# A decoder mixer on one core: low parts by accumulating transfer, layer 0's memory keys as split products, and three convolution taps moved from TensorE to VectorE

## The chip, the cores and the metric

The kernel runs as one program on one core of a Trainium2 chip. The core has TensorE (matrix products, "PE" in the profile; its weight loads are "PEld"), VectorE ("DVE"), ScalarE ("ACT"), GpSimd ("POOL"), SyncE ("SP", which here only issues transfers) and 16 DMA engines. The metric is the device time of one execution in microseconds (us), the median over several runs.

## The reference, cut to what matters

Two residual layers over a sequence of 512 positions with 1024 channels, all in f32; each layer has a mixer, a cross-attention into 256 memory tokens and a gated FFN. The change lies in layer 0's mixer and in the work that is done beside it:

```python
z = h @ w_in                                   # 1024 -> 512 (pooling) + 512 + 512 (gated convolution)
u, glu_a, glu_b = split(z)
pooled = [window_mean_minus_self(u_group_i, w) for w in (2, 4, 8, 16)]
ya = einsum(pooled, pool_w) * pool_scale
gl = glu_a * sigmoid(glu_b)
cv = causal_dwconv(gl, dw_w) + dw_b            # 31 taps on each of 512 channels
yb = silu(layernorm(cv, ln_g, ln_b))
x = x + concatenate([ya, yb]) @ w_out
# for the cross-attention of both layers, from the same memory tokens:
k, v = split(rmsnorm(mem, norm_mem_g) @ wkv)
```

## The kernel before

Activations lie transposed: a tile has 128 channels on the partitions and 512 positions along the row. To keep f32 accuracy, an operand `a` is split into a high part (a cast to the type fp32r) and a low part `a - high`; a product is then three TensorE products in fp32r, high x high, high x low and low x high (`mm3`, lines 179 to 181). A weight tile is 128 x 1024 f32 (512 KB). `load_raw` fetches it by a transfer of SP's queue into one of 4 buffers `wr`; `load_w` has ScalarE cast the high part (line 173, "wh") and VectorE subtract the low part (line 174, "wl"), each in one of 3 buffers, asked for 40 places ahead of its turn.

A second way to the low part is there and is used in the FFN only: ScalarE writes minus the high part's source, and a transfer of POOL's queue adds the weights from memory a second time.

```python
def early_parts():
    hi = wp.tile([P, WCOLS], F32R, tag="wh1", name=uid("wh1"), bufs=2)
    lo = wp.tile([P, WCOLS], F32R, tag="wl1", name=uid("wl1"), bufs=2)
    return hi, lo

def low_by_dma(lo, raw, src):
    act.mul(lo, raw, -1.0)                     # line 166; lo is fp32r: it keeps minus the rounded value
    pool.dma_start(lo, src, accum_op=ALU.add)  # line 167
```

The mixer does this, in the order of the code: twelve projection tiles of 24 products each (`opening`, then `project`; b and a halves of four channel groups, then the four pooling groups); layer 0's memory keys (8 tiles) and values (8 tiles, with the four products of the pooling map between them); layer 1's memory keys and values (16 tiles), kept in memory for later; the first half of the output projection, whose operand is `ya` (8 x 12 products, in 16 steps); its second half, whose operand is `yb`. Layer 0's keys are taken as f32 products of the raw weights with the raw memory tile (`native`, line 362); layer 1's are split products.

The depthwise convolution runs beside all that. Three channel groups and most taps of the fourth are VectorE instructions of 128 x up to 512 elements (line 934, `convolve`). The taps in `PE_TAPS` of the fourth group are TensorE products with a diagonal matrix (`tap_products`, line 945; ScalarE builds the diagonal, line 944), added to the rest at line 950. The code deals out VectorE's taps by counts, `PACE`, a few after every weight tile; `left[0]` counts those still open. When none is open, the stages of `normalise` (the LayerNorm over the channels and the swish, lines 952 to 981) are called one after the other at the steps that `LATE` gives.

The program text is not the order in which the engines run. A planner takes, for each engine, the ready instruction that stands first in the text (an instruction can be given a place ahead of its turn, as above), and readiness includes a free buffer. Each engine then runs its list in that order.

Of the kernel before, what the change touches and what calls it, by code (L numbers as in the profile page):

```python
# [19 lines left out]
P = 128  # L20
T = 512
TB = T // P
D = 1024
KD = D // P
# [25 lines left out]
WCOLS = 1024  # L50
SLOTS = 55
AHEAD = 40
FIN_AHEAD = 2
K_NATIVE = (True, False)
MEM_AT = (3, 6, 8)
MLA_AHEAD = 3
PE_TAPS = [1] + list(range(31 - 4, 31))
PE_PACE = 2
PACE = (3, 3, 2, 3)
MEM1_AT = 10  # L60
# [5 lines left out]
EARLY = 150  # L66
# [39 lines left out]
def kernel(ctx: ExitStack, tc: tile.TileContext, a):  # L106
    nc = tc.nc
    vec, act, pe, pool, sp = nc.vector, nc.scalar, nc.tensor, nc.gpsimd, nc.sync
# [10 lines left out]
    def uid(s):  # L119
        count[0] += 1  # L120
        return f"{s}{count[0]}"

    def slot(name, dt=F32, shape=(P, T)):
        return sl.tile(list(shape), dt, tag="s", name=uid(name))

    def bank(name="ps", shape=(P, T)):
        return pp.tile(list(shape), F32, tag="ps", name=uid(name))

    def small(name, shape, bufs=2, dt=F32):
        return sm.tile(list(shape), dt, tag=name, name=uid(name), bufs=bufs)  # L130

    def f(t):
        return t.bitcast(F32)
# [6 lines left out]
    def col(name, i=0, n=1):  # L140
        c = _COLS[name] + i
        return con[:, c:c + n]
# [5 lines left out]
    def load_raw(src, n):  # L148
        raw = wp.tile([P, WCOLS], F32, tag="wr", name=uid("wr"), bufs=4)
        sp.dma_start(raw[:, :n], src)  # L150
        return raw

    def parts():
        hi = wp.tile([P, WCOLS], F32R, tag="wh", name=uid("wh"), bufs=3)
        lo = wp.tile([P, WCOLS], F32R, tag="wl", name=uid("wl"), bufs=3)
# [10 lines that stand above are left out]
        act.mul(lo, raw, -1.0)  # L166
        pool.dma_start(lo, src, accum_op=ALU.add)  # L167

    def load_w(src, n):
        raw = load_raw(src, n)  # L170
        hi, lo = parts()
        with tc.high_priority(offset=AHEAD):
            act.copy(hi[:, :n], raw[:, :n])  # L173
            vec.tensor_tensor(lo[:, :n], raw[:, :n], f(hi[:, :n]), ALU.subtract)  # L174
        return hi, lo

    def mm3(ps, ah, al, bh, bl, first, last, more=False):

        pe.matmul(ps, ah, bh, start=first, stop=False, skip_group_check=more)  # L179
        pe.matmul(ps, ah, bl, start=False, stop=False, skip_group_check=more)  # L180
        pe.matmul(ps, al, bh, start=False, stop=last, skip_group_check=more)  # L181
# [153 lines left out]
                src = self.raw[k // 2][:, k % 2, :]  # L335
                vec.tensor_tensor(src, src, mem_rb, ALU.mult)

    def memory_gain(layer, memn, mg, mh):
        for i in range(KD // 2):
            m = slot("mg", shape=(P, 2, MEM))  # L340
            h = slot("mh", F32R, (P, 2, MEM))
            l = slot("ml", F32R, (P, 2, MEM))
            for j in range(2):
                act.activation(m[:, j, :], memn[i][:, j, :], AF.Identity,
                               scale=col("norm_mem_g", layer * KD + 2 * i + j))
            act.copy(h, m)
            vec.tensor_tensor(l, m, f(h), ALU.subtract)
            for j in range(2):
                mg.append(m[:, j, :])
                mh.append((h[:, j, :], l[:, j, :]))  # L350
            yield

    def memory_kv(layer, mg, mh, keep, native, kt, vt):

        for hd in range(HX):
            ps = bank("kx", (P, 2, MEM))
            for j in range(2):
                src = a["xa_wk"][layer, 2 * hd + j]
                if native:
                    w = load_raw(src, D)  # L360
                    for k in range(KD):
                        pe.matmul(ps[:, j, :], w[:, k * P:(k + 1) * P], mg[k], start=k == 0, stop=k == KD - 1)
                else:
                    Linear(src, KD, ps[:, j, :]).run(mh, 0, KD)
                yield
            kt.append(keep(ps, (P, 2, MEM)))
        for half in range(2):
            ps = [bank("vx") for _ in range(MB)]
            for kk in range(KD // 2):
                wh, wl = load_w(a["xa_wv"][layer, half, kk], 2 * T)  # L370
                for j in range(2):
                    k = 2 * kk + j
                    c = slice(j * T, (j + 1) * T)
                    for m in range(MB):
                        h, l = mh[k]
                        s = slice(m * P, (m + 1) * P)
                        mm3(ps[m], h[:, s], l[:, s], wh[:, c], wl[:, c], k == 0, k == KD - 1)
                yield
            for m in range(MB):
                vt[m].append(keep(ps[m], (P, T)))  # L380
# [490 lines left out]
    def mixer(norm, nxt):  # L871
        mem = Memory()
# [45 lines left out]
        def convolve():  # L918

            todo = [list(range(CONV_K)) for _ in range(CT - 1)] + [[s for s in range(CONV_K) if s not in PE_TAPS]]  # L920
            last = -1
# [16 lines left out]
        def tap_products():  # L938

            ps = bank("tap")  # L940
            i = CT - 1
            for n, s in enumerate(PE_TAPS):
                dg = small("dg", [P, P], bufs=4)
                act.activation(dg, ident, AF.Identity, scale=col("conv_dw_w", (CONV_K - 1 - s) * CT + i))
                pe.matmul(ps[:, s:], dg, gl[i][:, :T - s], start=n == 0, stop=n == len(PE_TAPS) - 1)
                yield
            while left[0]:
                yield
            s = PE_TAPS[0]
            vec.tensor_tensor(cv[i][:, s:], cv[i][:, s:], ps[:, s:], ALU.add)  # L950
# [32 lines left out]
        cv = [sl.tile([P, T], F32, tag="cv", name=uid("cv"), bufs=CT) for _ in range(CT)]  # L983
        left = [CONV_K * CT - len(PE_TAPS)]
        conv = convolve()

        def taps(n):
            for _ in range(min(n, left[0])):
                next(conv)
# [18 lines left out]
        for n, (kind, i) in enumerate(order):  # L1008
            if n == 2:
                lin.run(norm.h, 0, RB_K)  # L1010
                rb = norm.wide()
                wait.append((kind, i, lin.run(norm.h, RB_K, KD)))
            else:
                wait.append((kind, i, (project if n else opening)(base[kind] + i)))
            if n == 0:
                act.dma_start(con[:, KD:], a["con"][:, KD:])
            if n == 1:
                lin = Linear(a["pc_in"][base[order[2][0]] + order[2][1]], KD)
                lin.load(0)
                norm.r = row_rate(a["xN"], TB, "rx")  # L1020
            elif n > 1:
                if n == MEM_AT[0]:
                    mem.rate()
                if n == MEM_AT[1]:
                    mem.scale()
                if n == MEM_AT[2]:
                    scaled = [], []
                    for _ in memory_gain(0, mem.raw, *scaled):
                        pass
                while len(wait) > 1:  # L1030
                    finish(*wait.pop(0))
                if gl:
                    taps(PACE[0])
        kv = [], [[] for _ in range(MB)]
        products = tap_products()
        steps = memory_kv(0, *scaled, keep_slot, K_NATIVE[0], *kv)
        scaled = [], []
        gains = memory_gain(1, mem.raw, *scaled)
        for n, _ in enumerate(steps):
            if n == 0:  # L1040
                finish(*wait.pop(0))
# [11 lines left out]
        kv = [], [[] for _ in range(MB)]  # L1053
# [2 lines left out]
        late = normalise()  # L1056

        def filler():
            for _ in memory_kv(1, *scaled, keep_whole, K_NATIVE[1], *kv):
                yield 2  # L1060
            for m in range(KD):
                lin = Linear(a["pc_out"][m][:, :CT * P], CT)
                lin.run(cat, 0, CT // 2)
                yield 1
                vec.tensor_tensor(x[m], x[m], lin.run(cat, CT // 2, CT), ALU.add)
                yield 1
# [3 lines left out]
        for step in filler():  # L1070
            if left[0]:
                if step == 2 or left[0] % 2:
                    taps(PACE[3])
                if not left[0]:
                    for _ in products:
                        pass
            else:
                due -= 1
            if not left[0] and due <= 0 and stage < len(LATE):
                next(late, None)  # L1080
                due = LATE[stage]
                stage += 1
        out.append(kv)
        taps(left[0])
        for _ in products:
# [365 lines left out]
```

## Time and profile before

| | |
|---|---|
| median of 3 runs | 1383.85 us (1382.74 to 1384.0) |
| the profiled execution: time, span | 1383.12 us, 1381.3 us |
| TensorE busy, mean granted clock | 1352.6 us (98%), 0.993 |
| VectorE, ScalarE, POOL busy | 1020.0, 748.8, 52.9 us |
| layer 0's memory keys on TensorE | 75.9 to 107.6 us |
| layer 1's memory keys and values | 132.7 to 177.7 us |
| output projection, first half | 177.7 to 203.3 us |

Times of day are counted from the span's start. A row of a stretch has, for each engine, its busy time and in brackets the number of its instructions, then the granted TensorE clock as a share of full speed, the share of the 16 DMA engines that is busy, and GB/s. A row of the order in time has start, length, engine, line, operation, output and inputs, and in square brackets what the engine waited for. Matmul lengths overlap: the rate is read from their starts.

### The profile page before, as it was taken

Reading aid. Unit: us, or ns where it says so; the run is one execution under the profiler, and the core shown is the slowest. Engines: PE = TensorE matmul, PEld = TensorE weight load, DVE = VectorE, ACT = ScalarE, POOL = GpSimd, SP = SyncE. Lnnn points to the kernel's source line nnn. Section 1 sums busy time; section 2 is a strip of 40 time slices with the busy share of each in tenths; the row PEclk is TensorE's granted clock in tenths of the full one; section 3 lists DMA queues with packets and bytes.
Section 4 is the critical chain, followed back from the end, with each engine's and each line's share of the span. In section 5 each row is a group of like instructions: output and inputs, shape, how many; then the busy total and the mean of one; then the engine's idle time right before and its main releaser. Section 6 shows DMA issues by size and latency. Waiting matters only on the chain.

```text
span 1381.3 us, 20270 instructions
## 1 busy us (share of the span) xinstructions
PE 1352.6 (98%) x7756; PEld 1168.1 (85%) x7756; DVE 1020.0 (74%) x1897; ACT 748.8 (54%) x1264; POOL 52.9 (4%) x71
## 2 busy tenths in 40 slices
PE   8999999999989999999999999999999999999997
PEld 6888978888879999999887776888887899999987
DVE  6999989554787777776869775755549777777765
ACT  6416456445655555554447786644556555555433
POOL 0000000001100000000000000000011000000000
PEclk9999999999999999999999999999999999999999
DMA  9335634118835545553321113321486455555421
GB/s 327 99 104 188 217 104 151 61 38 207 184 91 130 159 124 138 134 137 94 106 81 50 43 47 107 107 77 61 124 188 124 130 132 143 134 136 144 111 73 62
DMA packets 57265, 168.01 MB, mean 122 GB/s; under 512 B 6480, under 2 KB 8144, under 8 KB 57168
## 3 DMA queue, kind: packets, MB, share of 16 engines
q1 hardware_dynamic: 47664, 135.55, 30.6%
q0 software_dynamic: 7776, 28.32, 12.3%
q10 hardware_dynamic: 1728, 2.86, 0.6%
q8 instruction: 60, 0.98, 0.3%
q14 instruction: 37, 0.30, 0.1%
HBM read 162.50 MB, written 4.19 MB: 121 GB/s over the span
## 4 chain that ended last, share of the span: by engine, by line
PE 88%; DVE 8%; ACT 2%; issue 1%; DMA 0%; SPq 0%; DVEq 0%; ACTq 0%
PE lin L179 11%; PE lin L181 11%; PE lin L180 11%; PE xyz L179 8%; PE xyz L180 8%; PE xyz L181 8%; PE down L180 4%; PE down L179 4%; PE down L181 4%; DVE cv L934 3%; PE s L1273 1%; PE mpv L1310 1%; DVE wl L174 1%; PE t L1298 1%; PE vx L180 1%
## 5 line engine op out<-in xcount | busy, mean ns | idle before, releaser
L179 PE MATMUL xyz<-th,wh 128*128 128x256 f32 x816 | 230.8, 284 | 10.6 <-ACT q L737 10.6
L181 PE MATMUL xyz<-th,wl 128*128 128x256 f32 x816 | 231.5, 284 | 0.0
L180 PE MATMUL xyz<-tl,wh 128*128 128x256 f32 x816 | 231.3, 284 | 0.0
L173 ACT CAST wh<-wr 128x1024 fp32r<-128x1024 f32 (+3 forms) x120 | 112.7, 944 | 161.8 <-issue 60.6
L179 PE MATMUL lin<-hh,wh 128*128 128x512 f32 x432 | 171.0, 396 | 5.9 <-ACT hh L286 5.9
L179 PEld LDWEIGHTS xyz<-th,wh 128*128 128x128 f32 x816 | 155.7, 192 | 23.2 <-ACT q L737 14.9
L180 PE MATMUL lin<-hl,wh 128*128 128x512 f32 x432 | 169.7, 393 | 0.0
L181 PE MATMUL lin<-hh,wl 128*128 128x512 f32 x432 | 169.2, 392 | 0.2 <-DVE wl L174 0.2
L180 PEld LDWEIGHTS xyz<-tl,wh 128*128 128x128 f32 x816 | 156.8, 192 | 7.1
L174 DVE TENSOR_TENSOR wl<-wr,wh 128x1024 fp32r<-128x1024 f32 (+3 forms) x120 | 130.1, 1086 | 42.4 <-ACT wh L173 40.9
L181 PEld LDWEIGHTS xyz<-th,wl 128*128 128x128 f32 x816 | 156.7, 192 | 0.0
L565 DVE TENSOR_TENSOR wl<-ws,wh 128x1024 fp32r<-128x1024 f32 x68 | 83.3, 1225 | 61.4 <-ACT wh L564 47.9
L564 ACT CAST wh<-ws 128x1024 fp32r<-128x1024 f32 x68 | 71.3, 1049 | 103.9 <-PE xyz L180 101.3
L179 PE MATMUL down<-fh,dwh 128*128 128x512 f32 x256 | 101.9, 398 | 1.2 <-ACT dwh L218 1.2
L180 PE MATMUL down<-fl,dwh 128*128 128x512 f32 x256 | 102.0, 398 | 0.0
L181 PE MATMUL down<-fh,dwl 128*128 128x512 f32 x256 | 100.5, 393 | 0.5 <-DVE dwl L219 0.5
L179 PEld LDWEIGHTS lin<-hh,wh 128*128 128x128 f32 x432 | 81.6, 189 | 22.3 <-ACT hh L286 6.2
L180 PEld LDWEIGHTS lin<-hl,wh 128*128 128x128 f32 x432 | 81.5, 189 | 18.5 <-DVE hl L287 2.7
L181 PEld LDWEIGHTS lin<-hh,wl 128*128 128x128 f32 x432 | 81.5, 189 | 17.5 <-DVE wl L174 0.6
L167 POOL DMA_DIRECT2D wl<-in_ffn_up x54 | 46.9, 868 | 1058.2 <-ACT wl L166 1058.2
L934 DVE SCALAR_TENSOR_TENSOR cv<-a,con,cv 128x509 f32<-128x509 f32 (+25 forms) x115 | 79.4, 726 | 0.1
L670 ACT ACTIVATE c<-c 128x512 f32<-128x512 f32 x44 | 27.8, 632 | 58.5 <-DVE c L669 58.3
(404 smaller groups left out, 3152.1 us busy)
## 6 DMA issues: line engine op xcount, KB each, us to landing
wr<-in_ffn_up SPq DMA_DIRECT2D x88, 512.0 KB, 4.1
wl<-in_ffn_up POOLq DMA_DIRECT2D x54, 512.0 KB, 5.7
dr<-in_ffn_down SPq DMA_DIRECT2D x64, 256.0 KB, 4.2
wr<-in_xa_wk SPq DMA_DIRECT2D x16, 512.0 KB, 3.5
wr<-in_xa_wv SPq DMA_DIRECT2D x16, 512.0 KB, 4.3
wr<-in_xa_wq SPq DMA_DIRECT2D x16, 512.0 KB, 3.5
wr<-in_xa_wo SPq DMA_DIRECT2D x16, 512.0 KB, 3.5
wr<-in_ffn_down SPq DMA_DIRECT2D x16, 384.0 KB, 3.3
```

Source lines behind the costliest of these rows:

```text
L167: pool.dma_start(lo, src, accum_op=ALU.add)
L173: act.copy(hi[:, :n], raw[:, :n])
L174: vec.tensor_tensor(lo[:, :n], raw[:, :n], f(hi[:, :n]), ALU.subtract)
L179: pe.matmul(ps, ah, bh, start=first, stop=False, skip_group_check=more)
L180: pe.matmul(ps, ah, bl, start=False, stop=False, skip_group_check=more)
L181: pe.matmul(ps, al, bh, start=False, stop=last, skip_group_check=more)
L564: act.copy(hi[:, :n], raw)
L565: vec.tensor_tensor(lo[:, :n], raw, f(hi[:, :n]), ALU.subtract)
L670: act.activation(c, c, AF.Silu)
L934: vec.scalar_tensor_tensor(cv[i][:, s:], gl[i][:, :T - s], w, cv[i][:, s:], ALU.mult, ALU.add)
L1273: pe.matmul(ps[i], q[:, i * P:(i + 1) * P], k[:, :P * (i + 1)], start=True, stop=True)
L1298: pe.transpose(banks[b][:, c:c + P], prob[n][i][:, j * P:(j + 1) * P], ident)
```

## The change

1. In the mixer, from behind the opening tile to the end of the first half of the output projection, every second full-width weight tile that `load_w` fetches (the first, the third, ...) gets its low part by the accumulating transfer, in the two early buffers, with its instructions asked for 150 places ahead.
2. Layer 0's memory keys are taken as split products, as layer 1's are; the native form is gone.
3. `PE_TAPS` shrinks from five taps (1, 27 to 30) to two (1, 30). The three others are done by VectorE.

```diff
-K_NATIVE = (True, False)
-PE_TAPS = [1] + list(range(31 - 4, 31))
+PE_TAPS = [1, 30]
...
+    relief = [False, 0]
+
     def load_w(src, n):
         raw = load_raw(src, n)
+        if relief[0] and n == WCOLS:
+            relief[1] += 1
+            if relief[1] % 2:
+                with tc.high_priority(offset=EARLY):
+                    hi, lo = early_parts()
+                    act.copy(hi, raw)
+                    low_by_dma(lo, raw, src)
+                return hi, lo
         hi, lo = parts()
...
-    def memory_kv(layer, mg, mh, keep, native, kt, vt):
+    def memory_kv(layer, mh, keep, kt, vt):
...
-                if native:
-                    w = load_raw(src, D)
-                    for k in range(KD):
-                        pe.matmul(ps[:, j, :], w[:, k * P:(k + 1) * P], mg[k], start=k == 0, stop=k == KD - 1)
-                else:
-                    Linear(src, KD, ps[:, j, :]).run(mh, 0, KD)
+                Linear(src, KD, ps[:, j, :]).run(mh, 0, KD)
...
+            if n == 0:
+                relief[0] = True
             if n == 1:
                 lin = Linear(a["pc_in"][base[order[2][0]] + order[2][1]], KD)
...
-        steps = memory_kv(0, *scaled, keep_slot, K_NATIVE[0], *kv)
+        steps = memory_kv(0, scaled, keep_slot, *kv)
...
+        relief[0] = False
         out.append(kv)
         taps(left[0])
```

More of the change, by code (lines that the diff above doesn't have):

```diff
@@ L336, in scale, with memory_gain @@
                 vec.tensor_tensor(src, src, mem_rb, ALU.mult)
-    def memory_gain(layer, memn, mg, mh):
+    def memory_gain(layer, memn, mh):
         for i in range(KD // 2):
@@ L348, in memory_gain @@
             for j in range(2):
-                mg.append(m[:, j, :])
                 mh.append((h[:, j, :], l[:, j, :]))
             yield
-    def memory_kv(layer, mg, mh, keep, native, kt, vt):
+    def memory_kv(layer, mh, keep, kt, vt):
         for hd in range(HX):
@@ L1026, in mixer @@
                 if n == MEM_AT[2]:
-                    scaled = [], []
-                    for _ in memory_gain(0, mem.raw, *scaled):
+                    scaled = []
+                    for _ in memory_gain(0, mem.raw, scaled):
                         pass
@@ L1035, in mixer @@
         products = tap_products()
-        steps = memory_kv(0, *scaled, keep_slot, K_NATIVE[0], *kv)
-        scaled = [], []
-        gains = memory_gain(1, mem.raw, *scaled)
+        steps = memory_kv(0, scaled, keep_slot, *kv)
+        scaled = []
+        gains = memory_gain(1, mem.raw, scaled)
         for n, _ in enumerate(steps):
@@ L1058, in filler @@
         def filler():
-            for _ in memory_kv(1, *scaled, keep_whole, K_NATIVE[1], *kv):
+            for _ in memory_kv(1, scaled, keep_whole, *kv):
                 yield 2
```

## The prediction

> **What bounds the kernel now.** I read the page's busy shares and its chain first, then busy times by stage.
>
> ```profile
> PE 1352.6 (98%) x7756; PEld 1168.1 (85%) x7756; DVE 1020.0 (74%) x1897; ACT 748.8 (54%) x1264; POOL 52.9 (4%) x71
> PE 88%; DVE 8%; ACT 2%; issue 1%; DMA 0%; SPq 0%; DVEq 0%; ACTq 0%
> ```
>
> TensorE bounds the whole, with VectorE on 8% of the chain. The stretches below are: opening, projections (to 75.9), layer 0 memory keys (to 107.6), its values (to 132.7), layer 1 keys (to 155.9) and values (to 177.7), first half of the output projection (to 203.3). The last two rows are FFN stretches that are used later.
>
> ```profile
> core 0: us, PE busy (x) PEld busy (x) DVE busy (x) ACT busy (x) POOL busy (x), PEclk, DMA share, GB/s
> 0.00:20.00 20.00, 13.94 (x44) 9.05 (x45) 10.82 (x13) 15.27 (x29) 0.71 (x6) 1.00 0.92 338
> 20.00:40.00 20.00, 20.00 (x92) 16.57 (x91) 15.46 (x36) 11.22 (x22) 0.00 (x0) 1.00 0.81 278
> 75.90:107.60 31.70, 31.70 (x139) 26.20 (x138) 31.70 (x67) 6.23 (x10) 0.00 (x0) 1.00 0.36 116
> 107.60:132.70 25.10, 25.02 (x110) 20.08 (x110) 25.10 (x34) 17.21 (x27) 0.20 (x1) 1.00 0.56 190
> 132.70:155.90 23.20, 23.20 (x194) 23.16 (x193) 23.20 (x30) 11.13 (x14) 0.00 (x0) 1.00 0.75 226
> 155.90:177.70 21.80, 21.80 (x98) 18.05 (x97) 19.93 (x27) 9.61 (x12) 0.00 (x0) 1.00 0.56 183
> 177.70:203.30 25.60, 24.13 (x108) 19.06 (x107) 20.60 (x44) 13.63 (x23) 0.00 (x0) 1.00 0.29 94
> 325.00:380.00 55.00, 55.00 (x248) 45.50 (x248) 34.00 (x67) 33.65 (x45) 7.79 (x9) 1.00 0.88 196
> 401.70:406.60 4.90, 4.90 (x20) 4.61 (x21) 3.23 (x6) 1.36 (x3) 0.00 (x0) 0.50 0.36 119
> ```
>
> From 20 to 178 us TensorE never rests, and VectorE is full until 156. Both bind, so relief of VectorE alone brings little: only removed TensorE work shortens this stretch, if the operands stay on time.
>
> **Keys as split products.** The native form issues two records per product.
>
> ```profile
> 79.57 1.83 PE L945 MATMUL tap<-a,dg 128*128 128x511 f32 x4
> 90.58 17.43 PE L362 MATMUL kx<-mg,wr 128*128 128x256 f32 x80
> L179 PE MATMUL kx<-mh,wh x64: 278/283/283, 132.9 to 155.6; 128*128 128x256 f32 x64
> ```
>
> 80 records from 90.2 to 107.6 are 0.217 us each (the record's 17.43 us over 80 gives the same), so the 128 of layer 0 cost 27.8 us. Layer 1 already takes the split form: 3 x 64 products in 23.2 us, 0.121 each. Gain 27.8 - 23.2 = 4.6 us.
>
> **Taps.** The keys' stretch holds 31.7 us; less 27.8, five tap products took 3.9, or 0.78 each. The row above agrees (four records, two products, 1.83 us with the last one's tail). Three removed: -2.3 us. Together -6.9 us of TensorE work. Their three diagonal builds leave ScalarE, which is idle there.
>
> **VectorE.** Three taps come to it, and of the 1024-wide tiles in the mixer (11 projections, 16 keys, 16 values) every odd one loses its VectorE low part: 43 tiles, 22 by transfer, 21 by VectorE, against 11 + 8 + 16 = 35 before.
>
> ```profile
> L174 DVE TENSOR_TENSOR wl<-wr,wh 128x1024 fp32r<-128x1024 f32 x44 | 53.4, 1217 | 8.8 <-ACT wh L173 8.8
> L934 DVE SCALAR_TENSOR_TENSOR cv<-a,con,cv 128x509 f32<-128x509 f32 (+25 forms) x115 | 79.4, 726 | 0.1
> 77.60:106.20 28.60, 16.88 (x24) 1.00 0.36 113
> ```
>
> -14 x 1.22 + 3 x 0.73 = -14.9 us. But four low parts (4.9 us) enter the first keys' stretch, which becomes shorter while VectorE is full there. What gives way are taps: the last row counts 24 tap instructions while the windows of four key tiles are computed, where the code asks for 12 (3 a tile), so the planner pulls taps forward into gaps and a low part can take their place. Cost 0; without that cover up to 4.9 us.
>
> **What the three taps do to the order: the step on which I put most weight.** The tap count is 31 x 4 = 124 less those on TensorE: 119 before, 122 after. The code deals them out: 10 x 3 in the projections, 8 x 3 + 8 x 2 with layer 0's memory, 16 x 3 with layer 1's, in sum 118. Before, one is left at the first step of the output projection; one is odd, so that step takes it, and the LayerNorm stages begin there, spread over the projection's 16 steps. After, four are left; four is even, a step of that kind takes taps only when the number left is odd, so none is taken, the count never reaches zero, and no LayerNorm stage is issued inside the projection. All of them (mean, transposes, rate, spread, swish, splits) come behind its 96 products in the order of priority. The next products need their result, so the chain lies bare on TensorE. Its links before:
>
> ```profile
> 182.07 1.10 PE L962 MATMUL mean<-lacc,om 128*128 128x512 f32 x2 [1.47 <-DVE lacc L957]
> 183.20 2.48 DVE L966 TENSOR_TENSOR cv<-cv,mean 128x512 f32<-128x512 f32 x4 [0.68 <-PE mean L962]
> 187.40 1.48 DVE L970 TENSOR_TENSOR lsq<-lsq,lq 128x512 f32<-128x512 f32 x2
> 189.86 0.60 PE L241 MATMUL st<-ident,lsq 128*128 128x128 f32 x4
> 194.36 0.16 DVE L234 SCALAR_TENSOR_TENSOR lny<-lnt,lny 128x4 f32<-128x4 f32 x1
> 194.57 0.65 PE L268 MATMUL rb<-ident,lny 128*128 128x128 f32 x4
> 195.87 1.28 ACT L978 ACT_TABLE_LOAD   x1
> 197.16 2.94 ACT L978 ACTIVATE cv<-cv,con 128x512 f32<-128x512 f32 x4
> 200.51 0.62 ACT L218 CAST ybh<-cv 128x512 fp32r<-128x512 f32 x1
> 203.26 0.39 PE L179 MATMUL lin<-ybh,wh 128*128 128x512 f32 x1
> ```
>
> Mean to the last square sum 182.07 to 188.88 (6.8), transposes to the rate 189.86 to 194.52 (4.7), spread to the first cast 194.57 to 201.13 (6.6): 18.1 us with other work in between. Without it some 2.6 us less (four foreign 0.6 us VectorE pieces, and scraps), 15.5. I take 16.5, nearer the bare end, since fewer foreign pieces are left by then. The first low part adds 0.5.
>
> Then the clock. The trace shows one such rest:
>
> ```profile
> 401.69 0.58 PE L179 MATMUL xyz<-th,wh 128*128 128x256 f32 x1 [5.42 <-ACT q L737]
> ```
>
> After 5.4 us without work the granted clock is 0.50 for the next 4.9 us (the 401.7 row): half of it lost, 2.4 us. The Trainium skill, "TensorE: Matmul & The Clock Gate", section "Part 1: The HAM clock gate", says a window of some 3.4 us without activity halves the clock until about as much busy time has passed; the trace agrees.
>
> What goes away: the projection's stretch is 25.6 us, of which 96 products take 21.8 (as many took 21.8 in the row to 177.7), so the mean's wait of 1.5 and the LayerNorm's own products, 3.8 in all, are paid already. Tail: 16.5 + 0.5 + 2.4 - 3.8 = +15.6 us; bounds 14.6 and 17.2 if the order is as I read it, 0 if not.
>
> **The transfers.** Each costs ScalarE a second pass, POOL an issue, and the DMA engines a read and an addition.
>
> ```profile
> 329.42 1.05 ACT L166 ACTIVATE wl<-wr 128x1024 fp32r<-128x1024 f32 x1
> 330.76 0.86 POOL L167 DMA_DIRECT2D wl<-in_ffn_up  x1 [9.04 <-ACT wl L166]
> wl<-in_ffn_up POOLq DMA_DIRECT2D x54, 512.0 KB, 5.7
> wl<-in_ffn_up POOLq DMA_DIRECT2D x12, 512.0 KB, 7.7
> q0 software_dynamic: 1728, 6.29, 37.1%
> q1 hardware_dynamic: 2585, 9.17, 30.6%
> ```
>
> The fourth row and the two below are of 300 to 400 us. 22 negations and 8 new casts of 1.05 us are 32 us of ScalarE over 178 us; it has from 4.7 us (opening) to 25 us (first keys) free in each stretch, so 0. POOL has nothing else to do here. SP issues the same raw loads as before; those of the first keys are now given back by the split instead of by TensorE. But the two early buffers hold every second tile, so one comes back after four tiles, and cast, negation, issue and landing must fit into three tiles' time. Cast to issue is 2.4 us (a cast as long as the negation, 1.05, and 1.34 from the negation's start to the issue); landing 5.7 quiet, 7.7 in that loaded stretch: 8.1 to 10.1. Three key tiles are 3 x 23.2/8 = 8.7, three value tiles 3 x 21.8/8 = 8.2. So 0 to 1.9 us per four tiles at most; eight such rounds: 0 to 12 us. A transfer takes 37.1/12 = 3.1 us of all engines: four in 23.2 us of layer 1's keys add 0.53 to a share of 0.75, more than there is, though raw tiles can be fetched ahead. TensorE's order is planned by readiness and can let other products pass, so I take 2.5, nearer the quiet row.
>
> "DMA: Bandwidth & Descriptors" of the Trainium skill, section "Anatomy of one DMA", fits a transfer as 2.0 us + bytes/436e3. An estimate by it, for 512 KB, is 3.2 us, chain 5.5, stall 0; the trace differs, its landings are 5.7 and more, so by that sentence the sum would be 2.5 lower.
>
> Opening: the second projection is the first odd tile.
>
> ```profile
> 15.91 0.50 PE L181 MATMUL lin<-hh,wl 128*128 128x512 f32 x1 [0.21 <-DVE wl L174]
> ```
>
> Its low part was just in time by VectorE (0.2 late). By transfer, behind loads that keep the engines at 0.92, it comes some 8 to 10 us after the cast at 13.6, so near 23; the third projection, an even one (24 products, 5.4 us), can pass. 0 to 8 us; I take 1.5, as the other tile covers most. The memory loads behind (0.81) slip too, unseen by TensorE.
>
> **Sum.** -6.9 + 15.6 + 2.5 + 1.5 = +12.7 us on this execution's 1383.12 (span 1381.3): 1395.8. The median of the runs is 0.7 above it: 1396.5.
>
> **Rivals.**
> First, the order saves it (faster): the planner places the LayerNorm stages inside the projection after all, because TensorE takes what is ready.
>
> ```profile
> 238.04 0.35 PE L179 MATMUL sx<-kh,qh 128*128 128x256 f32 x1
> 238.58 0.40 PE L180 MATMUL lin<-hl,wh 128*128 128x512 f32 x1
> ```
>
> There, score products and a projection are mixed out of the code's order. For it; against it, the mean, the transposes and the spread stand exactly after 12, 42 and 60 projection products, as the code issues them: nothing overtook products that were ready. It decides if the mean stands before about the 50th of the 96; then the tail costs about 0 to 2: 1383.85 - 6.9 + 2.5 + 1.5 = 1381, down to 1377 without stalls.
> Second, the two early buffers bind fully: 12 instead of 2.5, and 4 at the opening: 1408.
> Third, everything cancels: the chain half hidden, 1383 to 1386.
>
> **How the numbers follow.** My forecast (1389 to 1402) 0.58; early buffers binding (above 1402) 0.15; order saves it 0.21; cancelling 0.06. Measurements of this kernel tell apart about 0.2%, 2.8 us: faster 0.20, same 0.07, slower 0.73. The range 1378 to 1406 leaves about 1 in 10 on each side.
>
> **What would show it.** Right: the mean's product behind all 96 products with the a half, a TensorE rest of 10 us or more before the first product with the swish half, and a clock below 1.00 there; keys of layer 0 in 23 to 24 us in 192 products; VectorE with rests before 156. The early buffers show as TensorE waits for the transfers. Wrong: if the mean stands among the projection's products, the tail falls away and with it the sign; if the first keys stay near 31 us, VectorE's low parts were late after all.

## The result, and the profile after

The changed kernel takes 1415.03 us (median of four runs, 1413.52 to 1416.18); the kernel before, on the same chip, 1383.92 us. The ratio is 1.0226, interval 1.0214 to 1.0239: 31 us slower. The forecast was 1396.5 us with a range of 1378 to 1406: right in direction, too small by 18.5 us.

The page of the changed kernel, its span, its busy shares and its chain:

```profile
span 1411.6 us, 20453 instructions
PE 1355.1 (96%) x7814; PEld 1172.9 (83%) x7814; DVE 1008.1 (71%) x1886; ACT 777.3 (55%) x1291; POOL 71.8 (5%) x93
PE 81%; issue 7%; DVE 4%; DMA 4%; ACT 3%; POOL 0%; SPq 0%; POOLq 0%; DVEq 0%; ACTq 0%
```

VectorE fell from 8% of the chain to 4%, and DMA, 0% before, now has 4%. TensorE has 2% less of a longer span: the time went into rests of TensorE. Its own waits in the mixer name them (engine and line, what was waited for: total, times, longest):

```profile
PE kx L190 <- DMA wl<-in_xa_wk: 6.0, 2, 4.5
PE lin L188 <- ACT ybh L227: 5.4, 1, 5.4
PE st L250 <- DVE lsq L973: 5.1, 1, 5.1
PE lin L190 <- DMA wl<-in_pc_in: 5.1, 1, 5.1
PE vx L189 <- DMA wl<-in_xa_wv: 3.6, 3, 1.4
PE rb L277 <- DVE lny L243: 3.2, 1, 3.2
```

Two families: three rows of waits for low parts that come by transfer (six waits, 14.7 us), and three inside the LayerNorm's chain (13.7 us). The line numbers are shifted, by nine at most: 188 to 190 are now the three products of `mm3`, 182 and 183 the ordinary cast and subtraction, 165 and 166 the negation and the accumulating transfer, and 177 the cast that goes with them.

Cut at the same events as before, the stretches of the changed kernel (engines' busy time, then granted clock, DMA share, GB/s):

```profile
20.00:40.00 20.00, 16.78 (x64) 13.59 (x65) 8.29 (x22) 9.54 (x11) 1.73 (x2) 0.83 0.81 235
84.20:110.70 26.50, 25.07 (x198) 23.92 (x197) 25.90 (x52) 14.49 (x16) 3.45 (x4) 1.00 0.80 205
110.70:136.00 25.30, 23.92 (x107) 19.46 (x106) 23.53 (x38) 20.09 (x27) 3.45 (x4) 1.00 0.95 252
136.00:191.80 55.80, 48.90 (x294) 43.75 (x293) 42.47 (x61) 28.89 (x40) 6.25 (x8) 0.94 0.87 231
191.80:213.50 21.70, 21.70 (x97) 17.99 (x96) 9.03 (x14) 5.24 (x9) 0.00 (x0) 1.00 0.30 98
213.50:230.50 17.00, 3.31 (x12) 1.61 (x11) 10.87 (x27) 8.38 (x13) 0.00 (x0) 0.70 0.10 31
230.50:254.10 23.60, 23.58 (x97) 19.13 (x97) 23.27 (x37) 18.53 (x31) 0.00 (x0) 0.93 0.37 121
```

The one stretch of before that the prediction did not show, the second half of the output projection:

```profile
203.30:225.10 21.80, 21.80 (x98) 18.03 (x97) 21.62 (x35) 17.16 (x30) 0.00 (x0) 1.00 0.45 144
```

| stretch | before | after | difference |
|---|---|---|---|
| opening and projections | 75.9 | 84.2 | +8.3 |
| layer 0's memory keys | 31.7 | 26.5 | -5.2 |
| layer 0's memory values | 25.1 | 25.3 | +0.2 |
| layer 1's memory keys and values | 45.0 | 55.8 | +10.8 |
| output projection, first half | 25.6 | 21.7 | -3.9 |
| LayerNorm's chain, bare | 0 | 17.0 | +17.0 |
| output projection, second half | 21.8 | 23.6 | +1.8 |
| the rest of the kernel | 1156.2 | 1157.5 | +1.3 |

The sum is +30.3 us, the difference of the two spans. The last three stretches of the mixer, +14.9 together, are the LayerNorm. From the start to 191.8 the kernel is 14.1 us late; the keys and the taps should have taken 6.9 off there, so, by this difference, the transfers cost 21.0: 8.3 in the opening and 12.7 behind it. The experiments test that.

### The profile page after: what moved, and what is told of

It reads as the page before. It is cut to its first block, busy times and chain, and to the rows that moved or that the text cites. A ratio compares the mean times of both kernels' runs of the same rounds, so it can differ in the third digit from the quotient of the medians.

```text
span 1411.6 us, 20453 instructions
## 1 busy us (share of the span) xinstructions
PE 1355.1 (96%) x7814; PEld 1172.9 (83%) x7814; DVE 1008.1 (71%) x1886; ACT 777.3 (55%) x1291; POOL 71.8 (5%) x93
## 3 DMA queue, kind: packets, MB, share of 16 engines
q0 software_dynamic: 10944, 39.85, 16.5%
## 4 chain that ended last, share of the span: by engine, by line
PE 81%; issue 7%; DVE 4%; DMA 4%; ACT 3%; POOL 0%; SPq 0%; POOLq 0%; DVEq 0%; ACTq 0%
PE lin L188 10%; PE lin L189 10%; PE lin L190 10%; PE xyz L188 8%; PE xyz L189 8%; PE xyz L190 8%; PE down L189 4%; PE down L188 4%; PE down L190 4%; DMA wl<-in_xa_wk 2%; DMA wl<-in_xa_wv 2%; PE s L1279 1%; PE mpv L1316 1%; PE t L1304 1%; PE fin L188 1%
## 5 line engine op out<-in xcount | busy, mean ns | idle before, releaser
L182 ACT CAST wh<-wr 128x1024 fp32r<-128x1024 f32 (+3 forms) x106 | 98.1, 929 | 139.4 <-issue 61.3
L183 DVE TENSOR_TENSOR wl<-wr,wh 128x1024 fp32r<-128x1024 f32 (+3 forms) x106 | 113.4, 1070 | 55.4 <-ACT wh L182 53.8
L165 ACT ACTIVATE wl<-wr 128x1024 fp32r<-128x1024 f32 x76 | 80.3, 1056 | 4.3 <-PE vx L189 4.3
L937 DVE SCALAR_TENSOR_TENSOR cv<-a,con,cv 128x507 f32<-128x507 f32 (+26 forms) x118 | 81.0, 732 | 0.2
```

The source lines that it names most:

```text
L937: vec.scalar_tensor_tensor(cv[i][:, s:], gl[i][:, :T - s], w, cv[i][:, s:], ALU.mult, ALU.add)
```

## The experiments

The theory after these rows: the even count of taps lays the LayerNorm's chain bare (some 15 us); the transfers come late, once in the opening and again among the memory keys and values (some 21 us); the split keys are a gain. The rivals: VectorE, with three more taps, is what makes things late; or the split keys cost as much as they save; or the transfers' place in the buffers, ScalarE's list or the DMA engines is to blame, which the first runs can't tell apart. Unless a text says otherwise, edits are made to the kernel before, with its line numbers (a loader of several ways shifts them by up to ten).

**The taps alone** (`taps_only`).

```diff
-PE_TAPS = [1] + list(range(31 - 4, 31))
+PE_TAPS = [1, 30]
```

> The kernel before with the tap list [1, 30] alone. Theory (order): four taps are left over at the output projection, the LayerNorm chain comes behind its 96 products and lies bare: tail +15 us (17.0 chain + 1.7 clock - 3.9 already paid, as in the changed kernel), taps -2.3 us, so about 1397 us, ratio 1.009. Rival (the order does not matter, the chain is only late because of what the transfers delayed): -2 us, ratio 0.998 to 1.000.

Measured: 1396.34 us, ratio 1.0091 (1.0076 to 1.0106), as the theory said. The mean's products and the projection's products of the a half, by tile (count, durations, first and last start):

```profile
L962 PE MATMUL mean<-lacc,om x2: 590/590/591, 196.3 to 196.7; 128*128 128x512 f32 x2
L179 PE MATMUL lin<-yah,wh x32: 389/389/389, 174.5 to 195.6; 128*128 128x512 f32 x32
```

The mean stands behind the last of the 96 products, and the swish half starts at 213.3 us. Three taps that cost VectorE 2.2 us move the end by 12.7 us, through a parity.

**The change with the LayerNorm put back** (`after_order`). Edit of the changed kernel:

```diff
-                if step == 2 or left[0] % 2:
+                if step == 2 or left[0]:
```

> The changed kernel with one condition altered, so that the four taps left are dealt out at the first steps of the output projection and the LayerNorm stages are issued inside it. Theory (order): the tail of 14 to 15 us goes, about 1400 us, 1.2% above the kernel before. Rival (the chain is late for other reasons, VectorE's backlog): less than 4 us go, above 1411 us.

Measured: 1398.45 us, ratio 1.0109 (1.0094 to 1.0124): 16.6 us less than the changed kernel. The mean now stands at 197.1, four microseconds into a projection that runs from 193.0 to 217.1. With the order mended, the kernel is still 15 us slower than before. All that follows is about those.

**The split keys alone** (`keys_only`).

```diff
-K_NATIVE = (True, False)
+K_NATIVE = (False, False)
```

> The kernel before with layer 0's keys as split products alone, every low part by VectorE. Theory (TensorE is the bound and taps give way to the eight new low parts): keys of layer 0 in 23 to 24 us of products, -4.6 us, about 1379 us, ratio 0.997. Rival (VectorE is the bound up to 118 us): eight low parts of 1.13 us, 9 us more of VectorE work, show as TensorE waits for VectorE, 0 to +4 us, ratio 1.000 to 1.003.

Measured: 1391.5 us, ratio 1.0056 (1.0039 to 1.0073): slower, the rival, and by more than its 4 us. TensorE does save its time at the keys: layer 0's values start at 103.3 instead of 107.6. But short waits of its weight loads for high and low parts (5.2 us in sum from 100 to 178, 0.9 before) take nearly all of it back. All but one of the projection's products stand from 177.3 on, against 177.7 before, and then TensorE waits for VectorE's sum. That wait, and the two stretches around it:

```profile
PE mean L962 <- DVE lacc L957: 7.3, 1, 7.3
160.00:180.00 20.00, 19.71 (x86) 15.41 (x84) 20.00 (x29) 8.46 (x12) 0.00 (x0) 1.00 0.51 164
180.00:200.00 20.00, 12.70 (x48) 9.70 (x49) 16.98 (x33) 4.69 (x8) 0.00 (x0) 0.83 0.25 82
```

VectorE was full up to 180, with eight low parts more than before (9.7 us at 1.22). The wait for its sum is 7.3 us instead of 1.5, and the clock behind it, 0.83 in the mean, takes about 2 us more, so the second half of the projection starts at 210.4 instead of 203.3. Without relief of VectorE, the faster keys are a loss; with the transfers beside them, they are the -5.2 of the table.

**VectorE relieved without a transfer** (`keys_taps8`): the split keys, with three taps more on TensorE instead of three fewer.

```diff
-K_NATIVE = (True, False)
+K_NATIVE = (False, False)
-PE_TAPS = [1] + list(range(31 - 4, 31))
+PE_TAPS = [1] + list(range(31 - 7, 31))
```

> Before with layer 0's keys as split products and three taps more on TensorE (eight) instead of three fewer; no transfers. keys_only was bound by VectorE (mean waited 7.3 us for its sum). Theory: VectorE is relieved of 2.2 us, TensorE pays 2.3 us that lay in the wait: the mean's wait shrinks to 5 us or less and the time falls from 1391.5 to 1387 to 1390. Rival (the builds on ScalarE or the order of the projection set it): no change or slower, 1391 to 1395.

Measured: 1391.72 us, ratio 1.0051 (1.0036 to 1.0066): the mean's wait shrank as expected, from 7.3 to 4.9 us, but the time did not move (the theory's wait, the rival's time). TensorE paid its 2.3 us for what it no longer waited, and the clock of 180 to 200 is 0.83 as before.

**The transfers alone** (`relief_only`). Keys native and five taps on TensorE, as before; only the first part of the change, cut here to its switch:

```diff
...
+        if relief[0] and n == WCOLS:
+            relief[1] += 1
+            if relief[1] % 2:
...
+            if n == 0:
+                relief[0] = True
```

> The kernel before with every second full-width tile's low part by accumulating transfer alone (35 such tiles, 18 by transfer; layer 0's keys stay native and have none). Theory (late transfers): about +8 us before the first keys, waits of 5 to 8 us in the values and layer 1's keys, little behind the first keys, whose native products need no low part: +13 us, 1394 to 1399 us. Rival (what was lost there came from the first keys' new low parts): at most +2 us, 1386 us.

Measured: 1410.7 us, ratio 1.0195 (1.018 to 1.021), 27 us slower: most of the whole change's loss, and 12 us beyond the theory's range. TensorE's waits:

```profile
PE vx L190 <- DMA wl<-in_xa_wv: 8.5, 4, 5.3
PE lin L191 <- DMA wl<-in_pc_in: 5.1, 1, 5.1
PE kx L191 <- DMA wl<-in_xa_wk: 4.2, 2, 3.4
```

Layer 0's keys start at 86.3 (76.1 before), and the span is 28.3 us longer. So the transfers cost some 18 us behind the opening. VectorE has three taps fewer here than in the changed kernel; it is not what makes them late.

The three parts alone make 12.7 + 7.9 + 27.1, some 48 us, the change 31. They are not additive: the 7.3 us wait of the split keys, for one, is not there when transfers relieve VectorE.

**One transfer alone,** the first (`first_only`).

```diff
...
+        if relief[0] and n == WCOLS:
+            relief[1] += 1
+            if relief[1] == 1:
...
```

> The kernel before with one single transfer: the low part of the first full-width projection tile, everything else as before. Theory (opening: the landing behind loads that fill the engines): TensorE waits 5 us for it and loses 2 to 3 us more at half clock: +6 to +8 us, 1390 to 1392 us. Rival (the 8 us before the first keys come from several transfers and from the casts on ScalarE that wait for the two early buffers): at most +3 us, 1386 us.

Measured: 1393.28 us, ratio 1.0072 (1.0057 to 1.0087): ten microseconds for one low part. In the order of time, its issue on POOL, TensorE's last row ahead of the product that needs it, that product, and the stretch after:

```profile
16.41 1.01 POOL L167 DMA_DIRECT2D wl<-in_pc_in  x1 [15.10 <-ACT wl L166]
...
19.60 0.40 PE L190 MATMUL lin<-hl,wh 128*128 128x512 f32 x1
25.13 0.79 PE L191 MATMUL lin<-hh,wl 128*128 128x512 f32 x1 [5.14 <-DMA wl<-in_pc_in]
25.10:29.10 4.00, 3.97 (x9) 3.14 (x10) 1.46 (x3) 0.93 (x1) 0.00 (x0) 0.50 0.84 314
```

Issued at 16.41, the low part landed 8.7 us later. From 18.34 on TensorE's list held six other products, 1.4 us of work; then it stood. The last row is the second part of the bill: the clock at 0.50 for some 4 us after the rest, about 2 us. A third is a wait of 0.8 us, just before, for the high part of the next tile, whose cast follows the transfer's two passes on ScalarE.

**The transfers begun later** (`late_start`). Edit of the kernel with the mended order:

```diff
-            if n == 0:
+            if n == 4:
                 relief[0] = True
```

> The kernel with the altered condition (after_order, 1398.5 us), and the transfers switched on only from the fifth projection on, behind the loads of the opening. Theory (the loaded engines at the opening make the first odd tile's low part 8 us late): -8 us, 1389 to 1391 us. Rival (the wait is only shifted into the keys and values, where the engines or buffers bind anyway): less than 3 us, above 1395 us.

Measured: 1393.84 us, ratio 1.008 (1.0065 to 1.0095), 4.6 us less, between the two expectations. The keys start at 77.6 instead of 85.4, but TensorE waits 7.9 us for their low parts (5.7 with the early start): a part of what the opening no longer loses is lost again behind it.

**The buffers exchanged** (`swap`). Tiles whose low part comes by transfer take the three ordinary buffers, VectorE's tiles the two early ones. Edit of the kernel with the mended order:

```diff
-                    hi, lo = early_parts()
+                    hi, lo = parts()
...
-        hi, lo = parts()
+        hi, lo = early_parts() if relief[0] and n == WCOLS else parts()
```

> after_order with the two buffer pools exchanged: the tiles with a transfer take the three ordinary buffers (back after six tiles), the VectorE tiles the two early ones. Theory (buffers): the chain of 10 to 12 us fits into five tiles of 2.7 to 2.9 us, waits for transfers in the keys and values go, -10 to -12 us, about 1387 us. Rival (the DMA engines themselves, at 0.9 and more of their time, cannot bring more): at most -3 us, above 1395 us. The opening's 8 us stay under both.

Measured: 1394.91 us, ratio 1.0086 (1.0069 to 1.0103): 3.5 us less, near the rival. The waits for low parts of keys and values fell from 9.1 to 2.3 us, so two buffers were too few for this landing; but a new wait came:

```profile
PE kx L188 <- ACT mh L355: 4.7, 1, 4.7
```

`mh` is layer 1's memory operand, which ScalarE scales and casts.

**Both** (`swap_late`): `n == 4` and the exchanged buffers.

> Exchanged pools and late start together. Theory (buffers, and the opening apart from them): both gains add up, 1377 to 1381 us, under the kernel before. Rival (DMA engines full): 1387 to 1391 us.

Measured: 1387.13 us, ratio 1.0032 (1.002 to 1.0043): the gains add up in part, to the rival's time. Keys start at 76.2, the opening's loss is gone; 3.5 us of waiting for `mh` stay, and 2.8 for low parts.

**Fewer transfers, or the memory operand earlier.** `late_quarter`, the kernel of the later start, with every fourth tile instead of every second:

```diff
-            if relief[1] % 2:
+            if relief[1] % 4 == 1:
```

> late_start with a transfer for every fourth tile instead of every second. Theory (two buffers, chain longer than three tiles): a buffer is now asked back after eight tiles, no wait for transfers; VectorE keeps 9 or 10 more low parts (11 us) and may become the bound as with the keys alone: 1380 to 1388 us. Rival (every transfer costs its share, whatever the buffers): half of late_start's remaining loss, no sign of VectorE as the bound.

Measured: 1389.34 us, ratio 1.0046 (1.0031 to 1.0061), a little above the theory's range. The mean waits 3.8 us for VectorE again: with few transfers VectorE binds, with many the transfers do.

`swap_late_mem`, the kernel with both edits, with layer 1's gains dealt out from an earlier step:

```diff
-MEM1_AT = 10
+MEM1_AT = 4
```

> swap_late with the preparation of layer 1's memory tiles called from step 4 of layer 0's memory work on instead of step 10. Theory (with the buffers no longer binding, TensorE's largest wait is for those tiles, whose casts stand on ScalarE behind casts for transfers): that wait of 3.5 us and the others beside it go, -3 to -5 us, 1382 to 1384 us. Rival (the DMA engines at 0.9 to 1.0 from 100 to 140 us set the pace): no more than -1 us, 1386 to 1387 us.

Measured: 1388.26 us, ratio 1.0038 (1.0024 to 1.0053), above both expectations: the wait for `mh` is gone, and one of 5.8 us stands for ScalarE's eviction of layer 0's keys (`kv`, line 387), of which the values' products need the bank. The wait moved. The same kernel with every third and with every fourth tile (`% 3 == 1` in `third_swap_mem`, `% 4 == 1` in `quarter_swap_mem`):

> swap_late_mem with a transfer for every third tile. If the DMA engines bind: 2 to 4 us under swap_late_mem, 1379 to 1382 us. If VectorE binds already (the mean waits for the last tap): equal or slower.

> swap_late_mem with a transfer for every fourth tile. If VectorE binds as with the keys alone, the mean waits 3 to 4 us for the last tap and the time is 1384 to 1387 us; if not, as third_swap_mem, 1379 to 1382 us.

Measured: 1400.17 (1.0123, 1.0108 to 1.0139) and 1388.37 us (1.0036, 1.0023 to 1.0049). Neither brought the gain that was expected: 5.4 and 4.2 us of waiting for `kv` in the one, 6.9 in the other. ScalarE's rows of the kernel with every fourth tile, then the product that waited for it:

```profile
119.34 1.04 ACT L177 CAST wh<-wr 128x1024 fp32r<-128x1024 f32 x1 [2.10 <-DMA wr<-in_xa_wk]
120.30 0.90 ACT L353 ACTIVATE mg<-mraw,con 128x256 f32<-128x256 f32 x2
121.11 1.04 ACT L165 ACTIVATE wl<-wr 128x1024 fp32r<-128x1024 f32 x1
122.05 0.60 ACT L355 CAST mh<-mg 128x512 fp32r<-128x512 f32 x1
122.56 0.58 ACT L387 COPY kv<-kx 128x512 f32<-128x512 f32 x1
123.19 0.79 PE L188 MATMUL vx<-wh,mh 128*128 128x512 f32 x1 [6.87 <-ACT kv L387]
```

ScalarE stood 2.10 us for a raw weight tile, and then did four other things before the 0.58 us eviction. Its list runs in order: an engine that is busy for 12.7 of the 20 us from 100 to 120 held TensorE for 6.9 us.

**Is it the place that was asked for?** (`swap_late_ahead`) The kernel with both edits, with the transfers' casts 40 places ahead of their turn, not 150:

```diff
-                with tc.high_priority(offset=EARLY):
+                with tc.high_priority(offset=AHEAD):
```

> swap_late with the transfers' casts asked 40 places ahead of their turn instead of 150, as the other tiles' casts are. Theory A (ScalarE's in-order list holds what remains: casts far ahead stand in front of the evictions and of the memory gains): the waits for mh and kv shrink below 1.5 us each and the time is 1383 to 1385.5. Theory B (the landing of the transfers holds it): with less head start the waits for wl grow above 4 us in sum and the time is 1389 or more. Theory C (VectorE or the mean's wait): no change, 1386.5 to 1388.

Measured: 1389.16 us, ratio 1.0035 (1.0022 to 1.0049). The waits are 4.1 us for `mh` and 4.7 us for low parts, as the second theory expected. The time can't be told apart from that of `swap_late` (1.0032), but the first theory's gain is not there: the long head start is not what holds TensorE.

**Or the transfers of layer 1?** (`swap_layer0`) The kernel with both edits, without them:

```diff
         late = normalise()
+        relief[0] = False
```

> swap_late without transfers in layer 1's memory keys and values. Theory A (the transfers of layer 1 cost): K1 and V1 fall back to 45 us, time 1381 to 1385. Rival (VectorE): the eight low parts that come back to VectorE bring back the mean's wait for its sum (7.3 us in keys_only), time 1388 to 1391.

Measured: 1382.33 us, ratio 0.999 (0.998 to 1.000), as the first theory said: 5 us less for eight transfers fewer, and no longer slower than before. ScalarE's rows in the kernel with both edits, then the stretch of 120 to 140 us in it and without layer 1's transfers:

```profile
126.13 1.06 ACT L165 ACTIVATE wl<-wr 128x1024 fp32r<-128x1024 f32 x1 [2.67 <-DMA wr<-in_xa_wk]
...
130.34 0.63 ACT L355 CAST mh<-mg 128x512 fp32r<-128x512 f32 x1
132.18 1.06 ACT L165 ACTIVATE wl<-wr 128x1024 fp32r<-128x1024 f32 x1 [1.21 <-DMA wr<-in_xa_wk]
```

```profile
120.00:140.00 20.00, 15.74 (x85) 12.97 (x85) 16.62 (x25) 15.05 (x26) 2.59 (x3) 1.00 1.00 266
```

```profile
120.00:140.00 20.00, 19.59 (x124) 17.41 (x124) 19.41 (x27) 14.24 (x23) 0.00 (x0) 1.00 0.59 178
```

The DMA engines' share, ahead of the last figure, is the point: 1.00 with the transfers and 0.59 without. Full engines deliver the raw tiles late, ScalarE stops for them twice, and the memory operand stands behind in its list. ScalarE did nearly the same work in both (15.05 and 14.24 us), TensorE 4 us more without. What is left there are 2.7 us of waiting for keys and 1.6 of the mean for VectorE.

**Only the projections' four transfers** (`swap_proj`): the line `relief[0] = False` stands ahead of layer 0's memory work.

```diff
+        relief[0] = False
         kv = [], [[] for _ in range(MB)]
         products = tap_products()
```

> swap_late with transfers only among the last six projection tiles of the opening stage, none in the memory work. VectorE gets three or four low parts less than keys_only's and none of the memory's transfers. Theory: the keys' gain is kept and the mean's wait stays at about 4 us: 1386 to 1389. Rival: the opening's transfers cost as first_only's did, about 4 us or more even late: 1391 or more.

Measured: 1390.67 us, ratio 1.0045 (1.003 to 1.006). The keys start at 76.3, so these transfers cost nothing; but the mean waits 6.8 us, nearly the 7.3 of the split keys alone. Against that kernel, VectorE has four low parts less (4.9 us), but also the change's three taps more (2.2 us), which the expectation left out: 2.7 us less in sum, and they brought the mean 0.5 us. In the first 40 us VectorE is busy for 24.1, against 26.3 before, so about 2 us were taken off where it has rests. That this is the whole of the difference was not tested.

**A few transfers in layer 1's values** (`swap_layer0_v2`, `swap_layer0_v4`). The version without layer 1's transfers, with two of them put back, and with four (there 15 stands for 11).

```diff
-            for _ in memory_kv(1, scaled, keep_whole, *kv):
+            for n, _ in enumerate(memory_kv(1, scaled, keep_whole, *kv)):
+                if n in (7, 11):
+                    relief[0] = n == 7
```

> swap_layer0 with two more transfers, on the first and the third of layer 1's value tiles. Theory (VectorE holds the last 1.6 us there, seen as the mean's wait for its sum): two low parts less, 2.4 us of VectorE, take that wait away, and with no stall of their own the time is 1380.5 to 1382. Rival (any transfer in layer 1 costs as much as it frees): 1382 to 1384.5, with a new wait for wl or for an eviction in the values.

> swap_layer0 with four more transfers, on every second of layer 1's value tiles. Theory (VectorE): the mean's wait is gone as in swap_layer0_v2, nothing more is gained, 1380.5 to 1382. Rival (transfers that follow each other stall): 1383 to 1385, with waits for wl or for evictions in the values.

Measured: 1384.4 (1.0004, 0.9995 to 1.0013) and 1385.77 us (1.0012, 1.0003 to 1.0021). In both the mean's wait is gone, as the theory said, and the rival's wait is there instead. TensorE's waits with two transfers (the profiled execution is the fastest of the eleven, 1382.18 us):

```profile
PE vx L189 <- DMA wl<-in_xa_wv: 3.0, 2, 2.0
PE kx L190 <- DMA wl<-in_xa_wk: 1.3, 2, 1.2
```

At the start of the values the share of the DMA engines rises from 0.72 to 0.93 (140 to 160 us). So neither two nor four transfers beside layer 1 bring more than they cost. No version tried is faster than before by more than can be measured; the best, without layer 1's transfers, is even with it.

## Why the prediction was right or wrong

**The order of the LayerNorm: right.** The parity step, its mechanism and its size: +15.6 predicted, +14.9 measured in the changed kernel, 16.6 by the run that takes it away. Bare chain 17.0 (16.5 and 0.5 predicted); first half 21.7 (21.8); the rest costs 1.8 of clock in the half that follows (2.4). The clock fell inside the chain already (0.70 there): the three rests of 5.1, 3.2 and 5.4 us are separate, and the second half begins at less than full speed. The clock rule that the prediction took from the Trainium skill, "TensorE: Matmul & The Clock Gate", section "Part 1: The HAM clock gate", agrees with these rows: the clock falls to 0.50 some 5.4 us after the mean's products, and 3.3 us into the second half it is back (in the opening, 4.0 us after the last product and 5.8 us after the next).

**Keys and taps: right in size.** -6.9 predicted for the keys' stretch; -5.2 measured, with 1.4 of it a wait for a low part. What the prediction didn't see is that the keys' gain depends on the transfers: alone it ends as a loss of 7.9 us, behind VectorE. That relief of VectorE alone brings little was one half of "Both bind"; the other half, that a faster TensorE alone brings nothing either, was not drawn.

**The opening: a step that failed.** The prediction said that the low part would come near 23; it came at 23.2. It took 1.5 instead of 8 because the third projection, with 24 products, could pass. Only eight of the 24 did: in the changed kernel's rows in the order of time they stand from the first row below to the second, and then TensorE stands.

```profile
15.23 0.50 PE L188 MATMUL lin<-hh,wh 128*128 128x512 f32 x1
17.75 0.40 PE L189 MATMUL lin<-hl,wh 128*128 128x512 f32 x1
23.22 0.79 PE L190 MATMUL lin<-hh,wl 128*128 128x512 f32 x1 [5.07 <-DMA wl<-in_pc_in]
```

5.1 us of rest, and some 2.7 us for products that start 0.43 us apart instead of 0.23 until 28.9, make 7.8 of the 8.3. The other sixteen products of the third projection (3.6 us at full speed) stand in TensorE's list behind the second's: their operands were there at 16.5, but the list is made ahead and is not changed when a transfer is late. No row carried the cover: that the planner would put all 24 ahead of a landing as late as this was assumed. One transfer alone shows the same order and the same 5.1 us. Whether all 24 in front would have brought the 1.5 was not run.

**The transfers behind the opening: the larger term that failed.** Bounds 0 to 12, 2.5 taken, 12.7 measured. (Four rounds of 1.4 us at the keys and four of 1.9 at the values would have made the upper bound 13.2.) The chain of cast, negation, issue and landing was right, the row for the landing was not. The landing in the changed kernel (minimum, median, maximum up to 200 us), and the queues from 100 to 190 us:

```profile
DMA to landing us min/median/max: 6.4/7.7/10.3
q0 software_dynamic: 1907, 6.91, 43.5%
q1 hardware_dynamic: 4025, 13.09, 42.3%
```

The quiet 5.7 never occurs here; the least is 6.4. The prediction had itself worked out that the transfers ask for more of the DMA engines than there is (0.53 on top of 0.75), and still went to the quiet row, trusting to other products that could pass. The estimate by the Trainium skill's "DMA: Bandwidth & Descriptors", section "Anatomy of one DMA", 3.2 us for the landing and no stall, is refuted by the same row. The two early buffers have their part too, as the longest wait shows (the last row is the stretch behind it):

```profile
147.16 1.05 ACT L177 CAST wh<-wr 128x1024 fp32r<-128x1024 f32 x1 [1.83 <-PE kx L189]
157.30 0.58 PE L190 MATMUL kx<-mh,wl 128*128 128x256 f32 x1 [4.54 <-DMA wl<-in_xa_wk]
157.00:161.00 4.00, 3.70 (x17) 3.70 (x18) 2.19 (x4) 0.00 (x0) 0.00 (x0) 0.50 1.06 279
```

ScalarE's cast had to wait until TensorE gave the buffer back. From there it took 2.3 us to the issue at 149.46 and 7.8 to the landing: 10.1, the upper end of the prediction's chain. But TensorE had only 5.5 us of other products until it stood at 152.7, about two tiles and not the three (8.7 us) that the prediction set against the chain. After the wait the clock is at 0.50. Waits of 9.6 us for keys and values and about 2 us of clock make 11.6 of the 12.7. How the waits divide between the buffers and the late landings stays open: the exchanged buffers took 3.5 us off, and a new wait stood in their place.

**ScalarE's second pass at 0, since it has time free:** wrong in kind. Its load was never the matter; its order was. That is shown in the experiments' rows of `kv` and `mh`; in the changed kernel itself TensorE waits for neither. The remark that the three diagonals leave ScalarE where it is idle was a misreading too: four of the five are built from 10 to 13 us, in the opening, and one at 81.6.

**The range.** The second rival, the early buffers binding, was the case that came true, with a chance of 0.15 and a time of 1408. It left out the larger ends: 4 at the opening instead of 8. With both upper ends and the tail's, 1383.12 - 6.9 + 17.2 + 12 + 8 = 1413.4, and 0.7 for the median: 1414.1, against 1415.0 measured. Measured, both passed their ends by a little (8.3 and 12.7) and the tail stayed under its own (14.9), so that the sum comes out so near is in part luck. The bounds were about right; they were treated as if independent, while one cause, landings under load that TensorE's list does not hide, drives both to their ends.

## What to carry to other kernels

A count that is dealt out by rest and parity is a schedule: before changing how many items there are, follow the count to the place where it must reach zero. A transfer that takes the place of arithmetic is to be costed with the landing of the load that it creates itself, against the time until its buffer is wanted, and raised by the clock's loss after every wait of about 5 us. Where the DMA engines are full (a share of 1.00 in `swap_late`), it also makes other loads late, and engines with time to spare then hold the bound one through the order of their lists. Where two engines bind, taking work off one shows as a wait for the other: the two have to be relieved together, and a range whose terms hang on one cause has to reach to the sum of their ends.

## What the runs showed of the hardware

One low part for which TensorE waited 5.1 us cost ten microseconds in all (`first_only`): the wait, and 0.50 of the clock for some 4 us behind it, are 7 of them.

An accumulating transfer of 512 KB is dear for the DMA engines: 43.5% of 90 us for 13 of them is 3.0 us of all sixteen each, while the loads' 13.09 MB, 25 such tiles, took 42.3%, 1.5 us each. And it slows the plain loads beside it: a raw tile of the memory keys and values lands in 3.5 and 3.6 us between 80 and 120 us of the kernel before, and in 5.5 and 6.5 in the version without layer 1's transfers, with the same twelve loads of raw tiles in these 40 us:

```profile
wr<-in_xa_wv SPq DMA_DIRECT2D x8, 512.0 KB, 3.6
wr<-in_xa_wk SPq DMA_DIRECT2D x4, 512.0 KB, 3.5
```

```profile
wr<-in_xa_wv SPq DMA_DIRECT2D x8, 512.0 KB, 6.5
wl<-in_xa_wv POOLq DMA_DIRECT2D x4, 512.0 KB, 7.9
wr<-in_xa_wk SPq DMA_DIRECT2D x4, 512.0 KB, 5.5
wl<-in_xa_wk POOLq DMA_DIRECT2D x2, 512.0 KB, 8.8
```

The bytes don't tell this: the stretch with a share of 1.00 moves 266 GB/s, while the opening of the changed kernel moves 335 at 0.93. A share near 1.00 with accumulating transfers in it is reached at fewer GB/s.
